# All pairs of heads in a written order on three engines; modulation sums kept out of the heads; the rotary swap on VectorE

## The chip, the cores and the metric

The kernel is one program on 1 core of one Trainium2 chip. The metric is the device time of one execution in microseconds (us); lower is better. Of the core's engines the text names TensorE (PE; its weight loads have a row of their own, PEld), VectorE (DVE), ScalarE (ACT), GpSimd (POOL) and SyncE (SP), which issues nearly all the loads. Before the change three runs took 1917.03 to 1919.51 us, with a median of 1918.83 us.

## The reference

The reference is a decoder trunk of two layers on one sequence of 256 tokens with 2048 features. Each layer has a mixer and a SwiGLU feed-forward network (FFN) with 5632 inner features. Shift, scale and gate of every sub-layer come from one conditioning vector c. Layer 0 mixes by pooling. After it, one set of keys and values is computed from a compressed latent of 512 features, and layer 1 attends to it with 16 heads of 128 + 64 features:

```python
for i in range(DEPTH):
    shift_m, scale_m, gate_m, shift_f, scale_f, gate_f = jnp.split(sc @ mod_w[i] + mod_b[i], N_MOD, axis=-1)
    if i == N_A:
        kv_shift, kv_scale = jnp.split(sc @ kv_mod_w + kv_mod_b, 2, axis=-1)
        h_kv = modulate(rmsnorm(x, kv_in_norm), kv_shift, kv_scale)
        kv = shared_kv(h_kv, w_dkv, kv_norm, w_uk, w_uv, w_kr, cos, sin)
    h = modulate(rmsnorm(x, norm_mix[i]), shift_m, scale_m)
    y = pool_mixer(...) if i < N_A else mla_mixer(h, kv, w_dq[j], q_norm[j], w_uq[j], w_o[j], cos, sin)
    x = x + gate_m[:, None, :] * y
    h = modulate(rmsnorm(x, norm_ffn[i]), shift_f, scale_f)
    x = x + gate_f[:, None, :] * swiglu(h, ffn_gate[i], ffn_up[i], ffn_down[i])
return rmsnorm(x, final_norm)
```

The rotary part of queries and of the shared key turns pairs of features: with t1 and t2 the halves of the 64, the result is (t1 cos - t2 sin, t2 cos + t1 sin).

## The kernel before

**Tiles and products.** A weight comes in units of 1 MB (a raw tile 128x2048). Each is split into an upper part, a rounded copy made by ACT (L374; L517 and L1362 are the same operation elsewhere), and a lower part, the rest, made by DVE (L376, L520, L1363). Activations are split in the same way, and a product is three products: upper by upper, upper by lower, lower by upper. One unit gives 24 matmuls of 128x512 on PE (L398).

**Stages.** The stages by time in the span are: pooling mixer and start of the modulation (0 to about 200 us), FFN of layer 0 (to about 890), a handover (to 938), then `keys_values(0..2)` with the first `hidden_q` (four pieces of the modulated hidden state, L540 and L558 to L560) and `w_dq` (to 998), `keys_values(3)` with the query latent (to 1010), the heads in 8 pairs (to 1098), the output projection `w_o` (to 1163), a second handover and the FFN of layer 1 (to the end).

**What sets the order.** Most of the program is ordered by a list scheduler from the written program, tile pools and priorities. Stretches inside `tc.manual_schedule(engines=ordered)` are kept as written on PE, ACT and DVE; in the kernel before, `then_attention` and the second handover are such stretches, and the heads aren't. Each engine runs its list in order: an instruction that waits holds all behind it. SP has such a list of loads too, and a load waits until the raw tile it fills has been used up.

**Modulation sums.** All but the first of the modulation matrices are reduced on DVE: a `Part` loads 1 MB and multiplies and sums it in one instruction (L211), 168 of them. They are a background list: `tick`, called once per weight unit, issues some of it at a rate that `plan(left, units)` or `release` sets, so that `left` remain after `units` ticks; `hold` stops it. When the last unit of a gate is in, the column is finished (L300), turned by PE (L292), copied by ACT (L294) and spread by DMA. `pending` holds work that `flush` issues at a later weight split.

**Handover.** Class `Handover` (L449 on) ends the FFN: the last down projection's products (L407), the last piece of the residual (L611, L612), the norm of that token half (ACT L427, DVE L470, POOL L472), scaling (L476; piece 0 on DVE, piece 1 on POOL), PE transposes (L482), modulated upper and whole parts (L490, L497, L499) and lower part (L503). `then_attention` continues with pieces 2 and 3 (L1183 to L1197), the key's rotary product (L1208, `key_part`) and the key latent (L1238 to L1253).

**Heads.** `project_heads(g)` loads and splits the query weights of two heads, makes the rotary product (12 matmuls, L1368 to L1370), copies it and its swapped halves by ACT (L843, four times L845), and the head products (L1288). `probabilities` is the softmax on ACT and DVE, `turned` transposes it (L1407), `output` multiplies it with the values. DVE finishes the rotation (L849, L850, L852).

## Time and profile before

| what | value |
|---|---|
| median of three runs | 1918.83 us (1917.03 to 1919.51) |
| profiled execution | 1918.19 us, of which the span is 1916.4 us |
| PE busy | 1862.8 us, 97% of the span |
| DVE busy | 1402.7 us, 73% |
| ACT busy | 850.2 us, 44% |
| DMA | 574.98 MB, mean 300 GB/s |

How to read it: the span is the time from the first to the last instruction, and the 1.8 us between span and execution time lie around it. Busy shares are means over stages with different limits, so a stage is read in a table of windows, and a wait is read in the timeline of one engine. There the columns are start, duration, engine, line, operation, output and inputs by the program's names, shapes and count. Where an engine stood idle first, square brackets give for how long and what ended it. Rows that follow on each other overlap a little, so a step is best read from one start to the next.

### The profile page before, as it was taken

How to read it: one execution, taken by the hardware profiler on the slowest of the kernel's cores; microseconds unless marked ns; L12 is line 12 of the kernel's file. 1: busy time of each engine (PE TensorE's matmuls, PEld its weight loads, DVE VectorE, ACT ScalarE, POOL GpSimd, SP SyncE). 2: the span in 40 equal slices, each digit the busy share in tenths (PEclk: the TensorE clock that was granted, in tenths of full speed). 3: DMA queues.
4: the chain of work that ended last, by engine and by line, in shares of the span. 5: the costliest groups of instructions: out<-in, count | busy, mean ns of one | idle time of the engine just before them, and what ended most of it. 6: DMA issues, size and time to landing. Idle time of an engine off the chain costs nothing.

```text
span 1916.4 us, 21930 instructions
## 1 busy us (share of the span) xinstructions
PE 1862.8 (97%) x8813; PEld 1507.8 (79%) x8813; DVE 1402.7 (73%) x1391; ACT 850.2 (44%) x958; POOL 26.9 (1%) x32
## 2 busy tenths in 40 slices
...
GB/s 399 398 418 417 368 364 333 319 299 361 357 344 332 327 330 326 332 373 274 212 371 291 293 278 194 397 318 335 260 284 240 241 240 239 249 222 205 220 198 44
DMA packets 86647, 574.98 MB, mean 300 GB/s; under 512 B 10977, under 2 KB 15505, under 8 KB 18321
## 3 DMA queue, kind: packets, MB, share of 16 engines
...
q14 instruction: 32, 0.26, 0.0%
q10 hardware_dynamic: 96, 0.02, 0.0%
...
## 4 chain that ended last, share of the span: by engine, by line
PE 69%; issue 22%; DMA 3%; DVE 3%; ACT 1%; SPq 0%; POOL 0%; POOLq 0%; DVEq 0%; ACTq 0%
PE ps L398 58%; DMA raw<-in_mod_w_dram 3%; PE ps L256 2%; PE ps L973 2%; PE ps L407 2%; PE ps L1288 2%; DVE raw L211 1%; PE ps L729 1%; PE ps L1197 1%; PE ps L540 0%; DMA raw<-in_mod_block_dram 0%; PE ps L196 0%; PE ps L948 0%; PE ps L770 0%; DVE hl L376 0%
## 5 line engine op out<-in xcount | busy, mean ns | idle before, releaser
L398 PE MATMUL ps<-hl,act 128*128 128x512 f32 x6744 | 1539.5, 390 | 1.9 <-DVE hl L376 1.0
L398 PEld LDWEIGHTS ps<-hl,act 128*128 128x128 f32 x6744 | 1263.0, 188 | 264.7 <-DVE hl L376 1.8
L376 DVE TENSOR_TENSOR hl<-raw,hl 128x2048 fp32r<-128x2048 f32 x289 | 661.1, 2289 | 253.2 <-ACT hl L374 252.5
L374 ACT ACTIVATE hl<-raw 128x2048 fp32r<-128x2048 f32 x289 | 553.1, 1918 | 647.8 <-PE ps L398 572.1
L211 DVE SCALAR_TENSOR_TENSOR raw<-raw,s_row 128x2048 f32<-128x2048 f32 x168 | 383.2, 2284 | 3.6 <-DMA raw<-in_mod_wt_dram 3.6
L256 PE MATMUL ps<-raw,s_strip 128*32 128x512 f32 x392 | 65.2, 760 | 34.6 <-DMA raw<-in_mod_w_dram 33.5
L698 DVE TENSOR_TENSOR act<-ps,act 128x512 f32<-128x512 f32 x96 | 64.5, 685 | 17.5 <-PE ps L398 17.5
L256 PEld LDWEIGHTS ps<-raw,s_strip 128*32 128x32 f32 x392 | 9.5, 121 | 70.0 <-DMA raw<-in_mod_w_dram 46.3
L784 DVE TENSOR_TENSOR x<-ps,x 128x512 f32<-128x512 f32 x32 | 22.1, 690 | 38.8 <-PE ps L398 38.8
L1288 PE MATMUL ps<-act,hl 128*128 128x256 f32 x384 | 49.6, 287 | 0.0
L1288 PEld LDWEIGHTS ps<-act,hl 128*128 128x128 f32 x384 | 48.3, 195 | 0.7 <-DVE act L1253 0.2
L407 PE MATMUL ps<-hl,act 128*128 128x512 f32 x192 | 47.0, 400 | 1.2 <-DVE act L503 1.2
L732 ACT ACTIVATE act<-ps 128x512 fp32r<-128x512 f32 x44 | 23.6, 594 | 50.0 <-PE ps L729 37.6
L407 PEld LDWEIGHTS ps<-hl,act 128*128 128x128 f32 x192 | 35.2, 188 | 10.7 <-ACT act L490 2.3
L263 DVE COPY t2k<-ps 128x256 f32<-128x256 f32 x4 | 1.7, 425 | 52.9 <-ACT t2k L262 52.9
L427 ACT ACTIVATE junk<-x 128x512 bf16<-128x512 f32 x23 | 14.5, 629 | 53.2 <-DVE x L612 37.6
L802 DVE TENSOR_TENSOR t2k<-ps,t2k 128x512 f32<-128x512 f32 x24 | 16.5, 689 | 28.5 <-PE ps L398 28.5
L798 ACT ACTIVATE t2k<-ps 128x512 f32<-128x512 f32 x24 | 14.2, 590 | 47.9 <-PE ps L398 47.9
L973 PEld LDWEIGHTS ps<-act,act 128*128 128x128 f32 x128 | 24.7, 200 | 11.6 <-issue 8.4
L696 ACT ACTIVATE act<-ps 128x512 f32<-128x512 f32 x32 | 19.1, 597 | 29.0 <-PE ps L398 28.8
L973 PE MATMUL ps<-act,act 128*128 128x256 f32 x128 | 31.9, 402 | 0.0
L733 DVE TENSOR_TENSOR act<-ps,act 128x512 fp32r<-128x512 f32 x44 | 28.1, 683 | 0.9 <-ACT act L732 0.9
...
## 6 DMA issues: line engine op xcount, KB each, us to landing
...
```

Of the source, the lines that this page charges most:

```text
L211: dve.scalar_tensor_tensor(out=r, in0=r, scalar=1.0, in1=s_row, op0=ALU.mult, op1=ALU.mult, accum_out=self.sums[:, self.n:self.n + 1])
L256: pe.matmul(self.bank[m * STRIP:(m + 1) * STRIP, :], lhsT=weights(k), rhs=r[:, k, i, :], start=first, stop=last)
L374: hi_ins = act.activation(hi, r, AF.Copy)
L376: lo_ins = dve.tensor_tensor(out=lo, in0=r, in1=hi.bitcast(F32), op=ALU.subtract)
L398: pe.matmul(banks[tok], lhsT=t_[:, i, k, tok * P:(tok + 1) * P], rhs=w[:, k, :], start=first and n < len(part), stop=last and n >= len(ord ...
L407: pe.matmul(bank, lhsT=t_[:, i, k, tok * P:(tok + 1) * P], rhs=w[:, k, :], start=first and n == 0, stop=last and n == len(order) - 1)
L698: dve.tensor_tensor(out=part, in0=banks[tok], in1=part, op=ALU.add)
L732: act.activation(m[:, 0, :, ts_], v, AF.Copy)
L733: dve.tensor_tensor(out=m[:, 1, :, ts_], in0=v, in1=m[:, 0, :, ts_].bitcast(F32), op=ALU.subtract)
L784: dve.tensor_tensor(out=x[:, tok, js], in0=banks[tok], in1=x[:, tok, js], op=ALU.add)
L973: pe.matmul(mixed[g][:, n % 2, :], lhsT=wp[g][:, k, ns], rhs=pool_all[g // 2][:, g % 2, k, :], start=k == 0, stop=k == KL - 1)
L1288: pe.matmul(pt[:, h, :], lhsT=w(h0 + h, k), rhs=t_[:, i, k, :], start=n == 0, stop=n == 3 * KL - 1)
```

## The change

1. The heads run in a written order: `heads_in_order` lays out scores, softmax in pieces (class `Softmax`), transposes, projection of pair g + 2, and `weighted` for pair g - 1, inside `manual_schedule`. The first units of the output projection run in halves of 12 matmuls around `weighted`. The query weights come as one contiguous tile per pair, rearranged on the host, with the rotary halves of the two heads in front.
2. The 16 units of the "mla" gate come ahead of the heads, and the heads have no ticks for modulation sums. Seven more units than before go into FFN 0, two more between the handover and the first rotary product; eight instead of five go into `w_o`.
3. The rotary swap goes by blocks of 64 rows and is made by DVE out of PSUM together with the sine product (two 64-row instructions and one cosine product); ACT's five copies are gone. `w_kr` comes as one contiguous 1 MB tile with the doubled columns in it.
4. ACT keeps plain copies of the transposed pieces 2 and 3 in the handover (`kept`, four copies of 128x512); `hidden_q` uses them, so 16 transposes are gone.
5. In the handover all scaling is on DVE, the first lower split is ahead of the first piece, and a step of the product order is exchanged. `hold` is one column earlier at the end of the FFN.
6. In the FFN the evacuation of a down product is put into `pending`, so it comes after the next split.

```diff
-FFN0_UNITS, MLA_UNITS, HEAD_UNITS, WO_UNITS, FFN1_UNITS = 95, 4, 16, 8, 60
+FFN0_UNITS, MLA_UNITS, DQ_UNITS, WO_UNITS, FFN1_UNITS = 93, 4, 5, 8, 60
-LATE, MLA_LATE, WO_LATE = 3, 5, 3
+LATE, MIX_LATE, MIX_DQ = 3, 14, 6
...
-            pending.append((0, spread))
+            pending.append((1, spread))
...
-            (dve if j == 0 else pool).tensor_scalar(out=self.turned[tok, j][0], in0=x[:, tok, j * CH:(j + 1) * CH],
-                                                    scalar1=self.rstd[:, tok:tok + 1], scalar2=None, op0=ALU.mult)
+            dve.tensor_scalar(out=self.turned[tok, j][0], in0=x[:, tok, j * CH:(j + 1) * CH],
+                              scalar1=self.rstd[:, tok:tok + 1], scalar2=None, op0=ALU.mult)
...
-                if last and j == ND - 1:
+                if last and j == ND - 2:
                     hold()
...
-                    elif i == 0:
-                        act.activation(x[:, tok, js], banks[tok], AF.Copy)
                     else:
-                        dve.tensor_tensor(out=x[:, tok, js], in0=banks[tok], in1=x[:, tok, js], op=ALU.add)
+                        pending.append((0, lambda bank=banks[tok], sums=x[:, tok, js]: gather(bank, sums, i == 0)))
...
-        act.activation(t_[:, 0, :], bank, AF.Copy)
-        for r in range(0, P, HALF):
-            act.activation(t_[r:r + HALF, 1, :], bank[r ^ HALF:(r ^ HALF) + HALF], AF.Copy)
+        for r in range(0, P, ROPE):
+            other = slice(r ^ ROPE, (r ^ ROPE) + ROPE)
+            dve.tensor_tensor(out=t_[r:r + ROPE, 1, :], in0=bank[other], in1=sin_t[other], op=ALU.mult)
+        dve.tensor_tensor(out=t_[:, 0, :], in0=bank, in1=cos_t, op=ALU.mult)
         return t_
     def rope_end(t_, dsts):
-        dve.tensor_tensor(out=t_[:, 1, :], in0=t_[:, 1, :], in1=sin_t, op=ALU.mult)
-        dve.tensor_tensor(out=t_[:, 0, :], in0=t_[:, 0, :], in1=cos_t, op=ALU.mult)
...
-    plan(n_all + MLA_LATE, FFN0_UNITS)
+    n_all -= n_mix
+    plan(n_all + MIX_LATE, FFN0_UNITS)
...
         split_upper(w[0])
+        split_lower(w[0])
         run(h.old(0))
...
-        run(b0[2], a1[2], b1[0], b1[1])
+        run(a1[2], b0[2], b1[0], b1[1])
...
+            for pt, dst in zip(pts, kept[-1]):
+                act.activation(dst, pt, AF.Copy)
...
-    release(n_all, MLA_UNITS)
+    release(n_all + MIX_DQ, MLA_UNITS)
...
-        pts = turned_pieces(pieces)
-        if len(hmx) < ND - 1:
+        pts = turned_pieces(pieces) if len(hmx) < 2 else kept[len(hmx) - 2]
+        if len(hmx) < 1:
             pieces = scaled(rstd, len(hmx) + 1)
...
-    plan(n_all - n_mix - WO_LATE, HEAD_UNITS)
+    plan(n_all, DQ_UNITS)
...
+        for g in range(pairs + 1):
+            if g < pairs:
+                sps = [scores(heads[g], h) for h in range(HG)]
+            if g >= 2:
+                behind[:] = [output(g - 2, banks.pop(g - 2)).ins]
+            if g < pairs:
+                soft[g] = [Softmax(sp) for sp in sps]
+                soft[g][0].masked()
...
+            if w:
+                split_upper(w)
+            if g < pairs:
+                soft[g][1].masked()
+            if g >= 1:
+                for s_ in soft[g - 1]:
+                    s_.turned()
+            if w:
+                split_lower(w)
+            if g + 2 < pairs:
+                heads.append(new_heads(g + 2))
+                t_ = rope_start(rope_products(*uq[g + 2]))
+            if g < pairs:
+                for s_ in soft[g]:
+                    s_.exponentials()
+            if g + 2 < pairs:
+                head_products(heads[g + 2], *uq[g + 2])
+            if g < pairs:
+                for s_ in soft[g]:
+                    s_.normed()
+            if g + 2 < pairs:
+                rope_end(t_, [(all_rows, heads[g + 2].qrT)])
+            run(fill[:half])
+            if g >= 1:
+                banks[g - 1] = weighted(heads[g - 1], soft.pop(g - 1))
+            run(fill[half:])
```

How the instructions move is shown at three places. The first is ACT around the transposes of `hidden_q(0)`, between the products of `w_uk` and `w_uv` of the third group of keys and values. The eight rows L558 and L559 make that piece's modulated whole and upper parts. Before, hl_6487 is the upper split of that group's `w_uv` and hl_6592 that of the first `w_dq`:

```order
L374 ACTIVATE hl_6487<-raw_6485 128x2048
L1280 ACTIVATE act_6283<-ps_6349 128x512
L374 ACTIVATE hl_6592<-raw_6586 128x2048
L1289 ACTIVATE act_6385<-ps_6400 128x512
L1289 ACTIVATE act_6385<-ps_6426 128x512
L558 ACTIVATE t2k_6467<-ps_6452,cols 128x256
L558 ACTIVATE t2k_6471<-ps_6452,cols 128x256
L559 ACTIVATE act_6466<-t2k_6467 128x256
L559 ACTIVATE act_6466<-t2k_6471 128x256
L558 ACTIVATE t2k_6475<-ps_6457,cols 128x256
L558 ACTIVATE t2k_6479<-ps_6457,cols 128x256
```

Now hl_6518 is the split of the same `w_uv`, and hl_6604 that of `w_dq`:

```order
L1297 ACTIVATE act_6415<-ps_6431 128x512
L1297 ACTIVATE act_6415<-ps_6457 128x512
L558 ACTIVATE t2k_6498<-ps_6483,cols 128x256
L558 ACTIVATE t2k_6502<-ps_6483,cols 128x256
L559 ACTIVATE act_6497<-t2k_6498 128x256
L559 ACTIVATE act_6497<-t2k_6502 128x256
L558 ACTIVATE t2k_6506<-ps_6488,cols 128x256
L558 ACTIVATE t2k_6510<-ps_6488,cols 128x256
L559 ACTIVATE act_6497<-t2k_6506 128x256
L559 ACTIVATE act_6497<-t2k_6510 128x256
L374 ACTIVATE hl_6518<-raw_6516 128x2048
L374 ACTIVATE hl_6604<-raw_6599 128x2048
```

On PE the first product with hl_6518 is still the next instruction after the eight transposes of `hidden_q(0)`; the two splits have gone from ahead of the eight ACT instructions to behind them.

The second place is where PE goes from the last group's `w_uv` (L398) to the first rotary product of the queries, on PE and on DVE. Before, PE:

```order
L398 MATMUL ps_6846<-hl_6855,act_6173 128x512 x8
L398 MATMUL ps_6846<-hl_6856,act_6173 128x512 x4
L1368 MATMUL ps_6896<-act_6836,hl_6891 128x256
L1369 MATMUL ps_6896<-act_6836,hl_6890 128x256
L1370 MATMUL ps_6896<-act_6836,hl_6890 128x256
```

and DVE ahead of that pair's rotation, where L1363 are lower splits of query weights and L1253 is the query latent's lower part:

```order
L211 SCALAR_TENSOR_TENSOR raw_6852,sums_6588<-raw_6852,s_row 128x2048
L1363 TENSOR_TENSOR hl_6891<-raw_6888,hl_6890 128x512
L1363 TENSOR_TENSOR hl_6891<-raw_6888,hl_6890 128x1024
L1253 SCALAR_TENSOR_TENSOR act_6836<-ps_6826,vcol,act_6836 128x256
L1363 TENSOR_TENSOR hl_6944<-raw_6941,hl_6943 128x512
L1253 SCALAR_TENSOR_TENSOR act_6836<-ps_6826,vcol,act_6836 128x256
L1363 TENSOR_TENSOR hl_6944<-raw_6941,hl_6943 128x1024
L1253 SCALAR_TENSOR_TENSOR act_6836<-ps_6831,vcol,act_6836 128x256 x2
L1363 TENSOR_TENSOR hl_7045<-raw_7039,hl_7044 128x512
L1363 TENSOR_TENSOR hl_7045<-raw_7039,hl_7044 128x1024
L850 TENSOR_TENSOR t2k_6909<-t2k_6909,cos_t 128x256
```

Now, PE, where L292 turns the column of the "mla" gate:

```order
L398 MATMUL ps_6848<-hl_6855,act_6199 128x512 x8
L398 MATMUL ps_6848<-hl_6856,act_6199 128x512 x4
L292 MATMUL ps_6893<-con,cols 16x128
L1370 MATMUL ps_6901<-act_6838,hl_6890 128x256
L1371 MATMUL ps_6901<-act_6838,hl_6889 128x256
L1372 MATMUL ps_6901<-act_6838,hl_6889 128x256
```

and DVE, where L300 finishes that column and L1459 are the lower splits of the first three pairs' query weights:

```order
L211 SCALAR_TENSOR_TENSOR raw_6851,sums_5661<-raw_6851,s_row 128x2048
L1261 SCALAR_TENSOR_TENSOR act_6838<-ps_6828,vcol,act_6838 128x256 x2
L1459 TENSOR_TENSOR hl_6890<-raw_6887,hl_6889 128x1536
L1261 SCALAR_TENSOR_TENSOR act_6838<-ps_6833,vcol,act_6838 128x256 x2
L1459 TENSOR_TENSOR hl_6948<-raw_6945,hl_6947 128x1536
L300 TENSOR_TENSOR cols<-sums_5661,vcol 128x16
L1459 TENSOR_TENSOR hl_6998<-raw_6995,hl_6997 128x1536
L850 TENSOR_TENSOR t2k_6914<-ps_6901,sin_t 64x256 x2
L851 TENSOR_TENSOR t2k_6914<-ps_6901,cos_t 128x256
```

The turn of the gate's column, which stood inside the heads, now stands right ahead of the first rotary product, and its column comes on DVE behind the second pair's lower split.

The third place is ACT at the end of the first pair's softmax, ahead of its transposes. Before, L1400 is the division for the second head, L1388 the scores of the next pair, L1409 the copies of turned probabilities:

```order
L1388 ACTIVATE t2k_7103<-ps_7098 128x128
L1362 ACTIVATE hl_7274<-raw_7269 128x1024
L1388 ACTIVATE t2k_7122<-ps_7117 128x128
L1409 ACTIVATE t2k_7140<-ps_7136 128x384
L1362 ACTIVATE hl_7393<-raw_7385 128x512
L1400 ACTIVATE t2k_7024<-t2k_7024,sm_7034 128x128
L1362 ACTIVATE hl_7393<-raw_7385 128x1024
L1409 ACTIVATE t2k_7146<-ps_7142 128x384
```

Now L1411 is the division for both heads, L1396 the next pair's scores, L1419 the copies:

```order
L1405 ACTIVATE t2k_7017,soft_7019<-t2k_7017,soft_7018 128x128
L1405 ACTIVATE t2k_7017,soft_7019<-t2k_7017,soft_7018 128x256
L1297 ACTIVATE act_7037<-ps_7059 128x512
L1411 ACTIVATE t2k_7013<-t2k_7013,soft_7016 128x128
L1411 ACTIVATE t2k_7017<-t2k_7017,soft_7020 128x128
L1396 ACTIVATE t2k_7102<-ps_7092 128x128
L517 ACTIVATE hl_7117<-raw_7115 128x1536
L1396 ACTIVATE t2k_7106<-ps_7097 128x128
L1419 ACTIVATE t2k_7129<-ps_7125 128x384
L1419 ACTIVATE t2k_7135<-ps_7131 128x384
```

The divisions of the first pair have gone ahead of the next pair's scores and weight split.

## The prediction

> **What bounds the kernel now.** I read the page first, then a table of windows by stage, then the timelines of PE, ACT, DVE and POOL where a window showed PE idle. The page's row of PE:

> ```profile
> PE 1862.8 (97%) x8813; PEld 1507.8 (79%) x8813; DVE 1402.7 (73%) x1391; ACT 850.2 (44%) x958; POOL 26.9 (1%) x32
> ```

> The windows (length, busy time of each engine with its instructions, granted clock, DMA share, GB/s):

> ```profile
> core 0: us, PE busy (x) PEld busy (x) DVE busy (x) ACT busy (x) POOL busy (x), PEclk, DMA share, GB/s
> 200.00:890.00 690.00, 689.85 (x3089) 571.99 (x3088) 577.14 (x479) 285.87 (x227) 0.70 (x1) 1.00 0.88 339
> 890.00:938.20 48.20, 44.37 (x231) 35.63 (x230) 35.70 (x51) 33.00 (x60) 16.39 (x10) 1.00 0.44 147
> 938.20:998.10 59.90, 59.86 (x346) 52.20 (x345) 57.04 (x62) 44.59 (x69) 0.55 (x1) 1.00 0.97 377
> 998.10:1010.30 12.20, 12.20 (x83) 11.14 (x82) 11.77 (x14) 9.11 (x17) 2.46 (x1) 1.00 0.87 303
> 1028.80:1098.00 69.20, 66.79 (x437) 61.08 (x437) 66.55 (x142) 57.25 (x150) 0.61 (x1) 0.98 0.73 268
> 1098.00:1163.00 65.00, 65.00 (x288) 53.79 (x288) 42.85 (x35) 27.40 (x25) 0.00 (x0) 1.00 0.72 270
> ```

> PE has work in nearly every microsecond from 200 on. Where the change acts, it can win only 48.20 - 44.37 = 3.8 us in the handover, 69.20 - 66.79 = 2.4 us in the heads, a stretch of lower clock there (0.98), and the time of products that are taken out. Between 938 and 1010 it can only lose by waits: PE is full, and DVE has 59.90 - 57.04 + 12.20 - 11.77 = 3.3 us to spare.

> **The handover: -2.5 us.** PE's three large waits there (idle time and what ended it in brackets):

> ```profile
> 900.41 0.66 PE L482 MATMUL ps<-con,t2k 128*128 128x128 f32 x4 [1.41 <-DVE t2k L476]
> 903.97 0.66 PE L482 MATMUL ps<-con,t2k 128*128 128x128 f32 x4 [0.80 <-POOL t2k L476]
> 912.88 1.88 PE L407 MATMUL ps<-hl,act 128*128 128x512 f32 x7 [1.18 <-DVE act L503]
> ```

> What lies ahead of the first two, on POOL and DVE:

> ```profile
> 899.93 3.98 POOL L476 TENSOR_SCALAR t2k<-x,rstd 128x512 f32<-128x512 f32 x1
> ...
> 894.28 2.29 DVE L211 SCALAR_TENSOR_TENSOR raw<-raw,s_row 128x2048 f32<-128x2048 f32 x1
> ...
> 899.87 0.49 DVE L476 TENSOR_SCALAR t2k<-x,rstd 128x512 f32<-128x512 f32 x1 [0.69 <-POOL rstd L472]
> ```

> The modulation sum at 894.28 stands ahead of L611, with which the chain to the first scaling begins. `hold` one column earlier takes it away: 2.3 us for a wait of 1.41, so all of that goes. POOL's 3.98 us become one more 0.49 on DVE: the 0.80 goes. The third wait hangs on the lower part (DVE L503), behind ACT's whole part and DVE's own; DVE now has the scalings too, so I give it 0.3 of 1.18. That is 1.41 + 0.80 + 0.3 = 2.5. Bounds: 0.8 (only the POOL part) and 3.4 (all three).

> **The kept copies: +0.8 us.** ACT makes two copies of 128x512 from PSUM more for each of two pieces. The nearest row is an evacuation of that shape; the others are ACT's rows around the second piece, and the upper parts of the key latent, which the products of the keys wait for:

> ```profile
> 1008.81 0.61 ACT L1280 ACTIVATE act<-ps 128x512 f32<-128x512 f32 x1
> ...
> 925.09 1.93 ACT L1183 ACTIVATE act<-ps,cols 128x256 fp32r<-128x256 f32 x4 [2.25 <-PE ps L540]
> ...
> 930.58 0.60 ACT L1238 ACTIVATE junk<-ps 128x512 bf16<-128x512 f32 x1 [0.76 <-PE ps L1197]
> ...
> 935.76 1.57 ACT L1251 ACTIVATE act<-ps,vcol 128x256 fp32r<-128x256 f32 x4
> ```

> The first piece's 1.2 us fall into the 2.25 in which ACT waits. Of the second piece's 1.2 the wait of 0.76 takes its part; 0.44 are left, and they reach the four latent rows at 935.76. The order also puts the split of the first `w_uv` among these four, so three of them come a split later, while PE has other products for most of it; for that I take another 0.4. In all 0.8. Bounds: 0 and 2.4 (4 x 0.61).

> **Transposes: -1.65 us.** Sixteen of the 128x128 transposes are gone. Eight run from one start to the next group's in 967.61 - 966.82 = 0.79 us, 0.10 each:

> ```profile
> 966.82 1.03 PE L540 MATMUL ps<-con,t2k 128*128 128x128 f32 x8
> 967.61 5.74 PE L398 MATMUL ps<-hl,act 128*128 128x512 f32 x24
> ```

> **The third group's keys and values: +5.95 us, and 1.5 for the clock.** The order puts the upper split of `w_uv` behind the eight ACT instructions of `hidden_q(0)`; PE needs it right behind the transposes. Before:

> ```profile
> 963.44 1.92 ACT L374 ACTIVATE hl<-raw 128x2048 fp32r<-128x2048 f32 x1
> ...
> 967.51 1.02 ACT L558 ACTIVATE t2k<-ps,cols 128x256 f32<-128x256 f32 x2
> ...
> 970.54 1.93 ACT L374 ACTIVATE hl<-raw 128x2048 fp32r<-128x2048 f32 x1
> ```

> The eight take 970.54 - 967.51 = 3.03 us, and start when the first four transposes are done, 0.4 before the last; then comes the split, 1.92, and about 0.2 to reach PE: 3.03 + 1.92 + 0.2 - 0.4 = 4.75 us in which PE has nothing else in its list. The lower split follows on DVE. For DVE and for PE ahead of this:

> ```profile
> 944.93 2.28 DVE L211 SCALAR_TENSOR_TENSOR raw<-raw,s_row 128x2048 f32<-128x2048 f32 x1
> ...
> 963.45 2.28 DVE L376 TENSOR_TENSOR hl<-raw,hl 128x2048 fp32r<-128x2048 f32 x1
> ...
> 961.06 5.92 PE L1288 MATMUL ps<-act,hl 128*128 128x256 f32 x48
> ```

> The lower split takes 2.28, while PE has 8 matmuls of 5.74 / 24 = 0.24, 1.9 us: 0.3 more, signals included. Nine sums instead of six now stand on DVE between the first group and this split, five of them ahead of the lower split of the third `w_uk`. From 944.93: the key's rotation 1.2, five sums and two splits 7 x 2.21, about 1 of waiting for ACT: 962.6. PE is at its first lower product at 961.06 + 8 x 0.12 = 962.0: with the signal 0.9 late, as all of these move with PE. In all 0.9 + 4.75 + 0.3 = 5.95. Bounds: 4.5 (the ACT chain without signals) and 8 (each of the sums' delays in full). What is late next is what stands behind, the four `w_dq` units; they find their splits ready, because in the wait DVE and ACT catch up.

> A halved clock follows such a wait once in this trace, the wait of 1.97 us in the heads (PE rows, and the window after it):

> ```profile
> 1030.81 0.55 PE L1407 MATMUL ps<-con,t2k 128*128 128x128 f32 x3 [1.97 <-ACT t2k L1400]
> ...
> 1032.69 0.41 PE L1368 MATMUL ps<-act,hl 128*128 128x256 f32 x1
> 1032.90 0.41 PE L1369 MATMUL ps<-act,hl 128*128 128x256 f32 x1
> ...
> 1031.70:1035.00 3.30, 3.30 (x18) 3.30 (x17) 3.30 (x9) 2.63 (x10) 0.00 (x0) 0.50 0.79 315
> ```

> For some 3.4 us these matmuls start every 0.21 us instead of 0.12: 3.4 x (1 - 0.12 / 0.21) = 1.5 us are lost. The waits of 1.41 and 1.18 had no such stretch (clock 1.00 in their window). A wait of 4.75 is over twice as long as the one that did it, so I add 1.5 once. [...]

> **The gate's column ahead of the first rotary product: +2.2 us.** L292 waits for L300 on DVE, behind the second lower split L1459, which waits for the second upper split on ACT, behind an evacuation that waits for the first half of `w_uv`. PE has the other half to do, 12 x 0.24 = 2.9 us. Against it stand the evacuation of 0.61, a split of 1536 columns on ACT and one on DVE, which before are done in two pieces each:

> ```profile
> 1009.45 1.58 ACT L1362 ACTIVATE hl<-raw 128x512 fp32r<-128x512 f32 x2
> ...
> 1008.05 0.68 DVE L1363 TENSOR_TENSOR hl<-raw,hl 128x512 fp32r<-128x512 f32 x1
> ...
> 1009.04 1.22 DVE L1363 TENSOR_TENSOR hl<-raw,hl 128x1024 fp32r<-128x1024 f32 x1
> ```

> 0.61 + 1.58 + 0.68 + 1.22 and 0.4 for L300 and signals (an estimate) are 4.5: PE waits 1.6. If DVE still carries one of the two sums that it has more by here, some 1.2 of its 2.28 are added, 2.8. I take the middle, 2.2, and no half clock; bounds 1.6 and 4.5 (with one).

> **Heads: -3.5 and -0.8 us.** Ahead of the wait of 1.97 ACT has a split in front of the division:

> ```profile
> 1029.83 0.64 ACT L1362 ACTIVATE hl<-raw 128x512 fp32r<-128x512 f32 x1
> 1030.35 0.41 ACT L1400 ACTIVATE t2k<-t2k,sm 128x128 f32<-128x128 f32 x1
> ...
> L845 ACT ACTIVATE t2k<-ps 32x256 f32<-32x256 f32 x20 | 7.5, 375 | 0.3
> L211 DVE SCALAR_TENSOR_TENSOR raw<-raw,s_row 128x2048 f32<-128x2048 f32 x11 | 25.1, 2283 | 0.0
> ```

> Now the division is ahead of it, DVE has no sums in between (25.1 us less), and ACT loses its swaps. So this wait goes, with its half clock: 1.97 + 1.5 = 3.5. The later waits are small:

> ```profile
> 1068.34 0.33 PE L1407 MATMUL ps<-con,t2k 128*128 128x128 f32 x1 [0.26 <-ACT t2k L1400]
> 1078.06 0.70 PE L1414 MATMUL ps<-t2k,act 128*128 128x256 f32 x2 [0.17 <-ACT t2k L1409]
> ```

> They go too, 0.43, and about as much again in starts that come late without an idle row (an estimate): 0.8. Bounds for the heads together: 2.5 and 5.

> **Costed at nothing.** Seven more sums in FFN 0 are 7 x 2.28 = 16 us of DVE in a stage where it has 690 - 577 = 113 us free, and 7 MB on some 234 (339 GB/s x 690 us). Evacuations that come behind the next split hold their banks for 2.3 us longer; PE's 689.85 of 690 leave nothing to win and, if a bank were missing at each down product, 10 us and more to lose. Three more sums in `w_o` find 65 - 42.85 = 22 us of DVE. The swap on DVE adds 0.42 us a pair (two 64-row instructions and a cosine for a sine and a cosine), against 3 us a pair from the sums. The larger `w_kr` adds half a MB in a window with a DMA share of 0.44.

> **The sum.** -2.5 + 0.8 - 1.65 + 5.95 + 1.5 + 2.2 - 3.5 - 0.8 = +2.0. From the profiled execution, 1918.19 us (the span of 1916.4 and 1.8 around it, which stay), that gives 1920.2 us. The profiled execution stands 0.6 below the median shown, 1918.83. A measurement tells about 0.2% (3.8 us) from no change, so this is no change.

> **Rivals.**
> - *Faster.* The waits cost only themselves. The handover gives 3.4 instead of 2.5, the copies hide (-0.8), the third `w_uk` isn't late and the lower split comes in time (-1.2), the clock holds (-1.5), the gate's column costs 1.6 (-0.6), the heads give 0.7 more: 5.7 less, 1914.5. For it: DVE is less loaded in the heads and before; against it: the window 938 to 998 has no slack that would hide three of these.
> - *Slower.* DVE and the queue behind it decide from 945 on. It has 3.3 us to spare up to 1010 and gets two more sums, 4.4 us, and three more than now ahead of the first `hidden_q`; loads wait for the raw tiles these free, with DMA at 0.97. If DVE stays behind through `w_dq`, its lower splits come 1 us late three times, the wait at L292 is 3 and its clock is halved too: 3 x 1 + 0.8 + 1.5 = 5.3 more, 1925.5. It decides once DVE's backlog at the first `w_dq` unit is over 1.8 us, the 8 matmuls that PE can do without the lower split.
> - *It doesn't do what it says.* The scheduler's order keeps the waits in the heads, as ACT's scores of the next pair still depend on PE; then the heads' 4.3 are not won: 1924.5 with the two new waits, some 1917 if the scheduler's times were as wrong for those.

> **How the numbers follow.** The forecast has 0.45: 0.35 of it within 0.2%, 0.08 slower, 0.02 faster; its own range is 1916 to 1925. The faster rival has 0.27, the slower 0.20, the last 0.08 (half within, half slower). Faster 0.29, same 0.39, slower 0.32. The range reaches from beyond the faster rival's value, 1911.5, to beyond the slower one's, 1927.

> **What would show it.** In the changed profile, right: no bracket at L482 over 0.3 us; an idle of 4 to 5 us on PE ahead of the third `w_uv` (L398), released by ACT L374; a PE idle of 1.5 to 3 at L292; a half-clock stretch near 975 and none near 1030; DVE near full from 945 to 1010. Wrong: PE idle by less than 2 us at that `w_uv`, new idle time in FFN 0, or brackets above 0.5 us inside the heads.

## The result, and the profile after

The changed kernel takes 1927.97 us (median of five runs, 1927.82 to 1928.14). The kernel before, run beside it, takes 1918.76 us (five runs, 1914.87 to 1919.51). The ratio is 1.0052, with a 95% interval from 1.0041 to 1.0063: slower by 0.5%, 1 us beyond the upper end of the predicted range. The profiled execution takes 1927.86 us, 9.67 more than the one of before.

The page's row of busy times, after:

```profile
PE 1863.2 (97%) x8797; PEld 1508.1 (78%) x8797; DVE 1412.7 (73%) x1394; ACT 830.0 (43%) x904; POOL 20.9 (1%) x30
```

PE is busy for as long as before (1862.8 us); the span has grown from 1916.4 to 1926.1 us. So the time is idle time of PE. (Stretches in which its clock is halved count as busy: the 4.00 us at a mean clock of 0.57 further down are all busy.) The windows of the stages, after (the first is FFN 0, then the handover, the stretch to `w_dq`'s end, the query latent, the heads):

```profile
core 0: us, PE busy (x) PEld busy (x) DVE busy (x) ACT busy (x) POOL busy (x), PEclk, DMA share, GB/s
200.00:895.00 695.00, 692.06 (x3089) 571.19 (x3088) 593.10 (x494) 286.23 (x226) 0.70 (x1) 1.00 0.89 349
895.00:943.70 48.70, 45.38 (x235) 36.37 (x234) 35.73 (x52) 32.98 (x62) 10.35 (x8) 1.00 0.39 138
943.70:1010.50 66.80, 61.08 (x343) 53.43 (x344) 63.72 (x67) 41.12 (x64) 2.06 (x1) 0.97 0.96 371
1010.50:1022.50 12.00, 10.22 (x65) 8.89 (x63) 10.84 (x14) 9.95 (x14) 0.95 (x2) 1.00 0.80 273
1041.00:1107.00 66.00, 65.54 (x443) 60.50 (x442) 53.22 (x123) 47.62 (x123) 0.00 (x0) 1.00 0.36 133
```

PE now idles 2.9 us in FFN 0, where it idled 0.15; 3.3 in the handover, where it was 3.8; and 5.7 and 1.8 in two stretches that had none. The heads' idle time is down from 2.4 us to 0.46, and DVE has 53.22 of 66 us there where it had 66.55 of 69.

Every wait of PE of 0.4 us or more between 600 and 1125 us of the timeline, after (three dots stand for two rows that are like the first):

```profile
634.99 5.78 PE L398 MATMUL ps<-hl,act 128*128 128x512 f32 x24 [0.45 <-ACT hl L374]
...
835.90 22.10 PE L398 MATMUL ps<-hl,act 128*128 128x512 f32 x96 [0.45 <-ACT hl L374]
875.12 15.52 PE L398 MATMUL ps<-hl,act 128*128 128x512 f32 x66 [0.56 <-DVE hl L376]
891.22 3.48 PE L398 MATMUL ps<-hl,act 128*128 128x512 f32 x14 [0.58 <-DVE hl L376]
906.42 0.66 PE L482 MATMUL ps<-con,t2k 128*128 128x128 f32 x4 [1.74 <-DVE t2k L476]
914.92 2.56 PE L407 MATMUL ps<-hl,act 128*128 128x512 f32 x10 [0.88 <-DVE hl L520]
968.00 5.06 PE L1296 MATMUL ps<-act,hl 128*128 128x256 f32 x40 [1.07 <-DVE hl L376]
978.59 7.36 PE L398 MATMUL ps<-hl,act 128*128 128x512 f32 x24 [4.65 <-ACT hl L374]
1022.69 0.28 PE L292 MATMUL ps<-con,cols 128*16 128x128 f32 x1 [1.97 <-DVE cols L300]
1105.21 0.88 PE L1417 MATMUL ps<-con,t2k 128*128 128x128 f32 x6 [0.46 <-ACT t2k L1411]
```

The first stands four times (the two rows left out are at 680 and 725). It has an idle row of 0.45, but from PE's last start before it 0.73 us more than usual pass; for 875 and 891 that is 0.83 and 0.85.

To see where the time goes, take one PE instruction at the border of each stage and compare its start in the two timelines:

| from … to | before, us | after, us | difference | forecast |
|---|---|---|---|---|
| start … first unit of FFN 0 | 169.39 | 169.97 | +0.58 | 0 |
| … first product of the handover (L407) | 719.39 | 724.57 | +5.18 | 0 |
| … first product of the keys | 49.17 | 48.47 | -0.69 | -1.7 |
| … first rotary product | 72.21 | 79.71 | +7.50 | +8.0 |
| … first scores | 8.63 | 10.20 | +1.57 | 0 |
| … second pair's softmax transposes | 22.12 | 18.46 | -3.67 | -3.5 |
| … second handover | 122.01 | 121.22 | -0.78 | -0.8 |
| … end | 745.15 | 745.15 | 0.00 | 0 |

The first row isn't the change's: up to there the mean DMA share is 1.00 in both profiles (407 and 405 GB/s) and PE is busy for 131.47 of 169.39 us before and 129.81 of 169.97 after, and in the runs below it is -1.5 to +1.2 us without an edit in it. Three rows are off: FFN 0 by much, the 1.57 us behind the first rotary product, and the handover by 1.0. The 1.57 us are a second stretch of half clock. The windows behind the waits of 4.65 and 1.97 us, after:

```profile
978.00:983.00 5.00, 4.41 (x12) 3.53 (x13) 4.80 (x7) 2.34 (x2) 0.00 (x0) 0.66 1.01 421
1023.00:1027.00 4.00, 4.00 (x23) 4.00 (x22) 3.08 (x5) 0.27 (x1) 0.00 (x0) 0.57 0.99 347
```

### The profile page after: what moved, and what is told of

Read it like the earlier page. It is cut to its first block, busy times and chain, and to the rows that moved or that the text cites. A ratio compares the mean times of both kernels' runs of the same rounds, so it can differ in the third digit from the quotient of the medians.

```text
span 1926.1 us, 21857 instructions
## 1 busy us (share of the span) xinstructions
PE 1863.2 (97%) x8797; PEld 1508.1 (78%) x8797; DVE 1412.7 (73%) x1394; ACT 830.0 (43%) x904; POOL 20.9 (1%) x30
## 3 DMA queue, kind: packets, MB, share of 16 engines
q8 instruction: 69, 1.13, 0.2%
## 4 chain that ended last, share of the span: by engine, by line
PE 90%; DMA 4%; DVE 3%; ACT 1%; issue 1%; SPq 0%; POOL 0%; POOLq 0%; DVEq 0%; ACTq 0%
PE ps L398 75%; DMA raw<-in_mod_w_dram 3%; PE ps L256 2%; PE ps L1296 2%; PE ps L977 2%; PE ps L407 2%; DVE hl L376 1%; PE ps L729 1%; DVE raw L211 1%; PE ps L1475 1%; ACT hl L374 1%; PE ps L1208 1%; DMA raw<-in_mod_block_dram 0%; DMA raw<-in_w_uk_dram 0%; PE ps L196 0%
## 5 line engine op out<-in xcount | busy, mean ns | idle before, releaser
L398 PE MATMUL ps<-hl,act 128*128 128x512 f32 x6672 | 1526.9, 390 | 8.6 <-ACT hl L374 6.5
L398 PEld LDWEIGHTS ps<-hl,act 128*128 128x128 f32 x6672 | 1251.7, 188 | 272.1 <-ACT hl L374 8.4
L376 DVE TENSOR_TENSOR hl<-raw,hl 128x2048 fp32r<-128x2048 f32 x286 | 653.8, 2289 | 247.9 <-ACT hl L374 247.3
L374 ACT ACTIVATE hl<-raw 128x2048 fp32r<-128x2048 f32 x286 | 546.6, 1918 | 604.1 <-PE ps L398 433.8
L211 DVE SCALAR_TENSOR_TENSOR raw<-raw,s_row 128x2048 f32<-128x2048 f32 x168 | 383.0, 2285 | 2.0 <-DMA raw<-in_mod_wt_dram 2.0
L407 PE MATMUL ps<-hl,act 128*128 128x512 f32 x192 | 47.0, 398 | 1.1 <-DVE hl L520 0.9
L802 ACT ACTIVATE t2k<-ps 128x512 f32<-128x512 f32 x24 | 14.2, 590 | 71.7 <-PE ps L398 71.7
L407 PEld LDWEIGHTS ps<-hl,act 128*128 128x128 f32 x192 | 35.2, 188 | 10.6 <-ACT act L490 1.5
L520 DVE TENSOR_TENSOR hl<-raw,hl 128x2048 fp32r<-128x2048 f32 (+2 forms) x16 | 31.8, 1987 | 5.7 <-ACT hl L517 5.7
```

Source lines behind the costliest of these rows:

```text
L211: dve.scalar_tensor_tensor(out=r, in0=r, scalar=1.0, in1=s_row, op0=ALU.mult, op1=ALU.mult, accum_out=self.sums[:, self.n:self.n + 1])
L374: hi_ins = act.activation(hi, r, AF.Copy)
L376: lo_ins = dve.tensor_tensor(out=lo, in0=r, in1=hi.bitcast(F32), op=ALU.subtract)
L398: pe.matmul(banks[tok], lhsT=t_[:, i, k, tok * P:(tok + 1) * P], rhs=w[:, k, :], start=first and n < len(part), stop=last and n >= len(ord ...
L407: pe.matmul(bank, lhsT=t_[:, i, k, tok * P:(tok + 1) * P], rhs=w[:, k, :], start=first and n == 0, stop=last and n == len(order) - 1)
L520: dve.tensor_tensor(out=w[2][:, ks], in0=w[0][:, ks], in1=w[1][:, ks].bitcast(F32), op=ALU.subtract)
```

## The experiments

The times of each are set against the kernel before on the same chip; "FFN 0", "handover" and so on are the rows of the table above, worked out in the same way. Where no ratio is given, the kernel ran once, and its time has no interval.

**FFN 0: the sums alone, and the late evacuations alone.** The first experiment is the kernel before with seven more sums in FFN 0, the second the kernel before with the down products' evacuations put behind the next split, the third the changed kernel without that.

```diff
-LATE, MLA_LATE, WO_LATE = 3, 5, 3
+LATE, MLA_LATE, WO_LATE = 3, -2, 3
```

> The kernel before with one number changed: seven more modulation sums in FFN 0 (105 instead of 98, so fewer between the handover and the output projection). Theory A, the sums make FFN 0's waits: four waits of about 0.7 us at a split behind a Silu and two of about 0.85 at a DVE split, FFN 0 4 to 5 us longer than before, whole time about 1922. Theory B, the deferred evacuations make them: FFN 0 as long as before, whole time within 2 us of 1918.8.

```diff
-                    elif i == 0:
-                        act.activation(x[:, tok, js], banks[tok], AF.Copy)
                     else:
-                        dve.tensor_tensor(out=x[:, tok, js], in0=banks[tok], in1=x[:, tok, js], op=ALU.add)
+                        pending.append((0, lambda bank=banks[tok], sums=x[:, tok, js]: gather(bank, sums, i == 0)))
```

> The kernel before with one part of the change alone: the evacuations of FFN down products are deferred behind the next split. Theory A (the sums make FFN 0's waits): no waits in FFN 0, whole time within 2 us of 1918.8. Theory B (the deferral makes them): FFN 0 4 to 5 us longer, about 1923.5.

> The changed kernel without the deferral of the FFN down evacuations. The sums alone had cost FFN 0 2.95 us, all of the change 5.2. Theory A, the rest too is DVE's load near the end of FFN 0 (more sums per unit, since the stop comes a column earlier): FFN 0 stays at +5.2 within 0.5. Theory B, the deferral costs the rest once DVE is full: +3.

The sums alone: 1922.96 us, ratio 1.0023 (1.0013 to 1.0033). FFN 0 is +2.95, less than the 4 to 5 that theory A had: three of the four waits at a split on ACT are there (634.66, 679.84 and 725.02), the two on DVE at the end of the stage aren't. A new wait stands in the handover, where the last lower split comes late (PE's timeline with the sums alone):

```profile
896.78 8.46 PE L407 MATMUL ps<-hl,act 128*128 128x512 f32 x36 [2.75 <-DVE hl L376]
```

The evacuations alone: 1917.91 us, ratio 0.9992 (0.9983 to 1.0002), FFN 0 +0.01. The changed kernel without them: 1927.96 us, FFN 0 +5.16. So the evacuations cost nothing. It is the sums, and from 2.95 to 5.18 it is the sums together with the earlier `hold`, which leaves them one column less of the stage: that `hold` with 98 sums makes none of these six waits either (below).

**How seven sums cost FFN 0 5 us when DVE has 100 us free.** ACT's timeline around the wait at 634.99, after:

```profile
632.53 0.60 ACT L802 ACTIVATE t2k<-ps 128x512 f32<-128x512 f32 x1 [14.18 <-PE ps L398]
633.03 1.91 ACT L374 ACTIVATE hl<-raw 128x2048 fp32r<-128x2048 f32 x1
634.83 0.59 ACT L802 ACTIVATE t2k<-ps 128x512 f32<-128x512 f32 x1
```

The same place before:

```profile
621.21 1.92 ACT L374 ACTIVATE hl<-raw 128x2048 fp32r<-128x2048 f32 x1 [3.52 <-PE ps L398]
626.65 1.92 ACT L374 ACTIVATE hl<-raw 128x2048 fp32r<-128x2048 f32 x1 [3.52 <-PE ps L398]
631.18 0.60 ACT L798 ACTIVATE t2k<-ps 128x512 f32<-128x512 f32 x1 [2.62 <-PE ps L398]
633.90 0.60 ACT L798 ACTIVATE t2k<-ps 128x512 f32<-128x512 f32 x1 [2.12 <-PE ps L398]
```

L802 (L798 before) are the two Silus of a gate chunk, one for each token bank. After, ACT stands idle for 14.18 us until the first bank is finished, and the split that PE needs next stands behind the first Silu, although its weight, issued at 615.73, had landed 4.8 us later. It then starts 1.5 us before PE wants it and takes 1.91. Before, two splits have been done ahead of the Silus. The scheduler has changed the order because of the sums: no engine was short of time. ACT did not take the split ahead of the Silu that waited: 12.5 us pass from the landing of its weight (620.53) to its start (633.03), and ACT does nothing in them but that Silu.

The test writes the two Silus of the changed kernel in the other order, the bank that is finished last first:

```diff
-            nat[c] = []
-            for tok in range(NT):
-                sg = t2k([P, CH])
+            nat[c] = [t2k([P, CH]) for _ in range(NT)]
+            for tok in reversed(range(NT)):
+                sg = nat[c][tok]
                 act.activation(sg, gb[tok], AF.Silu)
-                nat[c].append(sg)
```

> The changed kernel, with the two Silus of a gate chunk written in the other order (the second token's bank, which is finished last, first), in both FFNs. In ScalarE's written order they then stand side by side again, with no split of a weight between them, although FFN 0 still holds 105 sums. Theory A (of FFN 0's +5.18 us, the four waits of 0.73 us over their usual length come from a split that stands between the two Silus and is kept by the second until TensorE's next bank is done; the two waits of 0.8 us at 875 and 891 us and what follows them come from VectorE's sums): the four waits are gone, FFN 0 costs +2.3 us (5.18 - 4 x 0.73), the time is 1925.0 us. Theory B (VectorE's load alone makes all six; a split that comes earlier on ScalarE is then late on VectorE): FFN 0 stays between +4.7 and +5.7 us, the time between 1927.4 and 1928.5 us. The bank that is read last is now read 0.6 us later, in FFN 1 as well, where 0 to 0.5 us is expected of that by both.

1924.68 us, ratio 1.0034 (1.0022 to 1.0046): 3.3 us less than the changed kernel. PE's timeline of it around 634, and the first wait that is left:

```profile
599.81 40.51 PE L398 MATMUL ps<-hl,act 128*128 128x512 f32 x178
...
873.24 15.53 PE L398 MATMUL ps<-hl,act 128*128 128x512 f32 x66 [0.56 <-DVE hl L376]
```

The four waits are gone, the two on DVE stay, and FFN 0 is +3.10, 2.1 less where 2.9 were expected. What is missing isn't in the waits. In this execution the clock was halved over the stage's first 6 us; in the changed kernel's profile it was so for half as long. The first 6 us of FFN 0 in the changed kernel, and in the one with the Silus turned (PE's clock is the number behind POOL's):

```profile
169.97:175.97 6.00, 6.00 (x20) 4.82 (x21) 5.86 (x12) 3.22 (x4) 0.00 (x0) 0.73 1.01 416
```

```profile
170.14:176.14 6.00, 6.00 (x14) 4.74 (x15) 5.86 (x12) 3.22 (x4) 0.00 (x0) 0.50 1.02 419
```

What goes with it is read at the start of the 97th product of the stage, set against the kernel before, whose clock was full there: +0.01 us in the changed kernel, +1.12 with the Silus turned. The 3.41 us of half clock in the changed kernel (0.50 from 169.75 to 173.16) cost no more by that product, as they take the place of two short waits for DVE's splits (0.38 and 0.58 us in the kernel before); the 6 us go with +1.12 here and with +1.13 in the run of the handover alone. That run has 98 sums and the Silus in the old order, this one 105 and the Silus turned, so it isn't these edits that choose. Behind that start FFN 0 is +1.98 instead of +5.17. So 3.2 us are ACT's order, four waits of 0.73 and a little more; 1.7 of the rest are the two waits on DVE (0.83 + 0.85) at the last splits. The run with the sums alone doesn't have these two, nor has the one with the earlier `hold` and 98 sums: it takes both.

Most of what remains of the 3.3 us in the whole time is the half clock at L292, which this profile doesn't have though its wait is 1.96 (clock 1.00 from 1021.2 to 1028; see the end).

**The handover alone.** The kernel before with the change's edits of the handover and `hold` one column earlier, without anything else:

```diff
-            (dve if j == 0 else pool).tensor_scalar(out=self.turned[tok, j][0], in0=x[:, tok, j * CH:(j + 1) * CH],
+            dve.tensor_scalar(out=self.turned[tok, j][0], in0=x[:, tok, j * CH:(j + 1) * CH],
...
-                if last and j == ND - 1:
+                if last and j == ND - 2:
                     hold()
...
+        split_lower(w[0])
         run(h.old(0))
...
-        split_lower(w[0])
         fs = h.old(1)
...
-        run(b0[2], a1[2], b1[0], b1[1])
+        run(a1[2], b0[2], b1[0], b1[1])
```

> The kernel before with the handover's edits alone (all scaling on DVE, first lower split ahead of the first piece, the exchanged step, the stop of the sums a column earlier). My prediction's term for it: handover 2.5 us shorter (2 to 3), whole 1917. Rival, DVE gets in each other's way there whatever the sums do: less than 1 us shorter, 1918.5 or more.

1918.79 us, ratio 1.0006 (0.9997 to 1.0015). The handover is -2.62, as forecast (-2.5). What it won went elsewhere: the sums that `hold` pushed on cost +2.10 ahead of the first rotary product, and the later heads +1.75. FFN 0 is +1.16, but +1.13 of it is the half clock over the stage's first 6 us in this execution, so the earlier `hold` alone costs nothing there. (The second pair comes 2.03 earlier, with a wait of 1.42 where it was 1.97 and no half clock behind it: 1.00 from 1031.5 to 1039.) In the changed kernel the handover is only -0.69, because DVE comes into it late: the last sums of FFN 0 push its splits and residual adds back, and the wait at L482 is 1.74, where it is 0.49 with 98 sums and the rest of the change, and gone with the handover's edits alone.

**The third group's keys and values.** First the changed kernel with the hidden state's transposes ahead of the third `w_uk`, so that the split of `w_uv` gets its time on ACT:

```diff
-        head_T(kT, KG, lambda h, k: hi[:, k, h * P:(h + 1) * P], lambda h, k: lo[:, k, h * P:(h + 1) * P], ckvT)
         if between:
             between()
+        head_T(kT, KG, lambda h, k: hi[:, k, h * P:(h + 1) * P], lambda h, k: lo[:, k, h * P:(h + 1) * P], ckvT)
```

> The changed kernel, with the transposes of hidden_q(0) ahead of the third group's w_uk products instead of between these and w_uv. Theory A, the split's place behind ACT's eight instructions makes the wait of 4.65 us: these now run under PE's products, and only an evacuation (0.6) and the split (1.9) with signals are left, a wait of 2.7; 1926, or 1924.5 if the clock stays up. Theory B, the late load or DVE's sums make it: the wait stays between 4 and 5, 1928.

1929.43 us, ratio 1.0050 (1.0035 to 1.0064): no gain; the stretch to the first rotary product is +11.78 instead of +7.50, and the 1.57 behind it are gone. PE's waits in it from 930 us on:

```profile
974.94 2.11 PE L398 MATMUL ps<-hl,act 128*128 128x512 f32 x8 [2.48 <-ACT hl L374]
979.64 5.53 PE L398 MATMUL ps<-hl,act 128*128 128x512 f32 x16 [2.58 <-DVE hl L376]
1011.04 0.66 PE L540 MATMUL ps<-con,t2k 128*128 128x128 f32 x2 [3.23 <-DVE sm L1247]
```

One wait on ACT became a smaller one, as theory A had it (2.7), and two on DVE. So DVE is late there as well. The 2.48 that stay on ACT come from the load of `w_uv`: it was issued at 964.05 and took 8.8 us to land, and the split starts 0.1 us after that, at 972.99. In the changed kernel the same load came as late. Its issue, its time from issue to landing, and ACT's splits of `w_uv` and `w_dq`:

```profile
965.06 0.33 SPq L387 DMA_DIRECT2D raw<-in_w_uv_dram  x1
...
raw<-in_w_uv_dram SPq DMA_DIRECT2D x1, 1024.0 KB, 8.5
...
976.62 3.72 ACT L374 ACTIVATE hl<-raw 128x2048 fp32r<-128x2048 f32 x2
```

So it landed at 973.57, 0.4 us before PE was through with its transposes (972.91 + 1.03). Of the 4.65 us, 3.05 (973.57 to 976.62) are ACT's order; about 1.6 would have stayed with any order, as the split takes 1.92. In the kernel before, this load was issued at 952.50. Next, three sums fewer between the handover and the first hidden state (six instead of nine). The last three of the sixteen tiles of the layer 1 mixer's gate are left out of the computation for it.

> The changed kernel with three sums fewer between the handover and the first hidden_q (6 instead of 9); the last 3 of the 16 tiles of the mla gate are left out of the computation. Theory A, DVE's backlog of sums sets the wait at the third w_uv: the wait of 4.65 us falls under 1.5, the 1.07 at the third w_uk goes, the clock stays up. Theory B, the order on ACT alone sets it: the wait stays at 4 to 5.

Its single run took 1917.21 us, without a wait of PE at that `w_uv`. The stretch to the first rotary product is -2.47 instead of +7.50, and the 1.57 behind it are gone: three sums, 6.9 us of DVE, cost 11.5 us. But this took away three things: DVE's time, 3 MB of loads, and with them ACT's order, which the scheduler wrote anew (the split of `w_uv` ahead of the eight copies of the hidden state). Two runs take them apart in part. In one, three of the nine sums cover 64 of 2048 columns, the loads stay, and so does ACT's order; in the other, three sums work on the tile that the sum before has used, so three loads go and DVE's time stays. The gate's values are then others.

```diff
+            js = slice(0, 64 if self.n in self.special else D)
-            dve.scalar_tensor_tensor(out=r, in0=r, scalar=1.0, in1=s_row, op0=ALU.mult, op1=ALU.mult,
+            dve.scalar_tensor_tensor(out=r[:, js], in0=r[:, js], scalar=1.0, in1=s_row[:, js], op0=ALU.mult, op1=ALU.mult,
```

> The changed kernel, with three of the nine sums between the handover and the first hidden state for the queries (tiles 3, 5 and 7 of the gate of layer 1's mixer) multiplied over 64 of their 2048 columns only: the 1 MB loads stay, some 6.6 us of VectorE go (3 x (2.29 - 0.08)). The order of ScalarE is the changed kernel's there: the upper split of the third w_uv stands behind the eight copies of the hidden state. The output of these tiles' gate leaves the other columns out. Theory A (the written order of ScalarE makes the wait at the third w_uv, VectorE's sums make the others): the 4.65 us there stay (4 to 5), the 1.07 ahead of it and the 1.97 at the gate's column are gone or under 0.6, no half clock behind the latter, and from the handover to the first rotary product it is +4 to +5.5 us instead of +7.50. Theory B (VectorE's backlog makes all three): the wait at the third w_uv is under 2 us as well, and the stretch at +1 us or less. Theory C (the loads, which move at some 420 GB/s there, make them): the three waits stay within 0.5 us, and the stretch at +6.5 to +8 us.

```diff
-            r = raw_t([P, D])
-            sync.dma_start(r, self.w[self.tiles[self.n] * P:(self.tiles[self.n] + 1) * P, :])
+            if self.n not in self.special:
+                self.r = raw_t([P, D])
+                sync.dma_start(self.r, self.w[self.tiles[self.n] * P:(self.tiles[self.n] + 1) * P, :])
+            r = self.r
```

> The changed kernel, with the same three sums made over a tile that the sum before has just used, so that VectorE has all nine sums and three loads of 1 MB are left out (the gate of layer 1's mixer is computed from other tiles there). ScalarE's order changes with it: the upper split of the third w_uv now stands ahead of the copies of the hidden state. Theory A (ScalarE's order, VectorE's sums): no wait of over 1.5 us on ScalarE at the third w_uv, but waits on VectorE of 2 to 4 us in all by the first rotary product, the wait at the gate's column (1.97 us, within 0.7) among them; from the handover to the first rotary product +1 to +4 us. Theory B (VectorE's backlog makes all): waits of 5 us and more in all, +5.5 us or more. Theory C (the loads): no waits, -2 us or less, as with three sums fewer altogether.

The two ran once each, 1925.37 us with the short sums and 1922.36 with the loads left out; the kernel before took 1915.51 beside them. PE's waits from 930 us on with the short sums:

```profile
975.38 8.11 PE L400 MATMUL ps<-hl,act 128*128 128x512 f32 x24 [4.65 <-ACT hl L376]
1020.22 0.28 PE L294 MATMUL ps<-con,cols 128*16 128x128 f32 x1 [1.96 <-DVE cols L302]
```

And with the loads left out:

```profile
1002.20 5.06 PE L1300 MATMUL ps<-act,hl 128*128 128x256 f32 x40 [1.09 <-DVE hl L379]
1010.07 0.44 PE L543 MATMUL ps<-con,t2k 128*128 128x128 f32 x2 [2.81 <-DVE sm L1251]
1018.61 0.27 PE L295 MATMUL ps<-con,cols 128*16 128x128 f32 x1 [0.36 <-DVE cols L303]
```

With 6.2 us less on DVE (the three sums took 0.22 us each instead of 2.29) and ACT's order kept, the 4.65 us stay and so does the wait at the gate's column (1.96); only the 1.07 at the third `w_uk` is gone (stretch +7.06, more than theory A's +4 to +5.5, as the gate's wait stayed and the 24 products behind the 4.65, part of them at half clock, took 8.11 us here instead of 7.36). So the two large waits aren't the time of these three sums. In the other run ACT's order is another, DVE has all nine sums, and the third `w_uv` lands at 966.50: the 4.65 is gone, and DVE's waits come to 1.09 + 2.81 + 0.36 (stretch +4.00, the upper end of theory A). Both mechanisms of the forecast are real: an order that holds the split back, and a backlog of DVE that costs some 4 us as soon as the order lets it through. Nine sums bring both, six neither. What the three loads do alone isn't shown, as no run leaves them out with ACT's order kept.

The 1.07 at the third `w_uk` is not DVE's backlog alone. In the changed kernel's profile ACT waits there for the load of `w_uk`, and DVE for ACT's split:

```profile
963.70 1.92 ACT L374 ACTIVATE hl<-raw 128x2048 fp32r<-128x2048 f32 x1 [2.56 <-DMA raw<-in_w_uk_dram]
...
965.66 2.29 DVE L376 TENSOR_TENSOR hl<-raw,hl 128x2048 fp32r<-128x2048 f32 x1 [0.62 <-ACT hl L374]
```

That load took 7.8 us to land. In the next run, with all nine sums and the same order up to there, it took 5.2, ACT and DVE have no such wait, and PE has none at that `w_uk`.

**The gate's column and the half clock.** The changed kernel with L292 and its copy in the second pair of heads:

```diff
-            pending.append((1, spread))
+            pending.append((1 if name != "mla" else 9, spread))
...
+            if g == 1:
+                flush()
             run(fill[:half])
```

> The changed kernel, with the turn of the mla gate's column (L292) moved from ahead of the first rotary product to the second pair of heads. Theory A: the wait of 1.97 us there goes and with it the half-clock stretch that follows, 3.5 us less: 1924.5. Theory B, the first pair's splits are as late as the column: a wait of over 1 us stays at the first rotary product, and the time is less than 1.5 us lower.

1923.43 us, ratio 1.0025 (1.0015 to 1.0034), 4.5 us less than the changed kernel. The stretch to the first rotary product is +4.77 instead of +7.50, and the +1.57 behind it is 0. By these rows it is 4.3 us, and 1.97 + 1.57 = 3.5 are the column's, as theory A had it; the rest is the 1.07 at the third `w_uk`, which this execution doesn't have, less a half clock that lasts longer behind the wait at the third `w_uv` (4.66; its 24 products took 7.97 us here and 7.36 in the changed kernel).

**Where the sums can go.** The last six runs keep the change and spread the sums otherwise; two of them also turn the Silus. First: 98 in FFN 0 as before the change, seven in the pairs of heads, the gate's column in `w_o`.

```diff
-LATE, MIX_LATE, MIX_DQ = 3, 14, 6
+LATE, MIX_LATE, MIX_DQ = 3, 21, 13
...
-            pending.append((1, spread))
+            pending.append((1 if name != "mla" else 0, spread))
...
+            pump(1)
...
-    plan(n_all, DQ_UNITS)
+    plan(n_all + 7, DQ_UNITS)
...
+            pump((1, 3, 5, 6, 7, 8, 8).count(g))
```

> The changed kernel with its sums spread differently and nothing left out: 98 in FFN 0 as before the change, 2 in the handover behind the modulated pieces, 7 up to the first hidden_q, 6 up to the first rotary product, 7 inside the pairs of heads (pairs 1, 3, 5, 6, 7 and two in the last round), the column's turn in the output projection. Theory A, DVE's load of sums makes the waits in FFN 0, at the third w_uv and at the first rotary product: FFN 0 within 0.5 us of before, under 1 us of waits at the third w_uv, none at the first rotary product, and the whole 6 to 7 us below the kernel before: 1912 to 1914. Theory B, the other parts (deferral, copies, swap) make them: the waits stay, and the sums in the heads add theirs: 1925 or more.

1916.51 us, ratio 0.9993 (0.9985 to 1.0002). FFN 0 is +0.77, the handover -1.95, the stretch to the first rotary product -2.53 without a wait; all of that is given back at one place, behind the heads (+4.61): an idle row of 3.78 us, 3.94 by the starts, with half clock behind it (a mean of 0.55 from 1102.2 to 1105.6). PE's timeline there, and DVE's:

```profile
1102.16 0.28 PE L292 MATMUL ps<-con,cols 128*16 128x128 f32 x1 [3.78 <-DVE cols L300]
```

```profile
1095.31 2.28 DVE L211 SCALAR_TENSOR_TENSOR raw<-raw,s_row 128x2048 f32<-128x2048 f32 x1
...
1097.52 2.29 DVE L211 SCALAR_TENSOR_TENSOR raw<-raw,s_row 128x2048 f32<-128x2048 f32 x1
...
1101.93 0.17 DVE L300 TENSOR_TENSOR cols<-sums,vcol 128x16 f32<-128x16 f32 x1
```

Taking the two sums of pair 8 to the query's first projections instead (five in the heads, eight there), without and with the other order of the Silus:

```diff
-    plan(n_all + 7, DQ_UNITS)
+    plan(n_all + 5, DQ_UNITS)
...
-            pump((1, 3, 5, 6, 7, 8, 8).count(g))
+            pump((1, 3, 5, 6, 7).count(g))
```

> The kernel with the sums spread again (98 sums in FFN 0, 2 in the handover, 7 before the first hidden state for the queries), with five sums in the pairs of heads (pairs 1, 3, 5, 6, 7) instead of seven (1, 3, 5, 6, 7, 8, 8), and the two that this takes out put with the query's first projections, which then hold 8. The gate's column transpose stays in the output projection. Theory A (the 3.94 us wait at that transpose, and the half clock behind it, come from the last two sums standing on VectorE right ahead of the column): the wait is gone, the part from the first transpose of weights of the second pair to the second handover falls from +4.61 us to between 0 and +0.7, the time is 1912.2 us (1916.5 - 4.3), faster than both kernels. Theory B (VectorE is full there as elsewhere, so two sums that are taken out of the last pairs come back as waits before the first rotary product): from the handover to the first rotary product it is +1 to +3 us instead of -0.58, and the time 1914.5 to 1917 us.

> The kernel with five sums in the heads, and the two Silus of a gate chunk in the other order. With 98 sums in FFN 0, one of the four waits of 0.7 us is left by the written order (a split between two Silus in two of the chunks instead of the seven). Theory A (the split between the Silus is what costs): 0.5 to 0.8 us less than the kernel with five sums and the old order, 1911.6 us if that one has 1912.2. Theory B (it is VectorE's load): no difference to it, within 0.3 us.

1919.12 us, ratio 1.0007 (0.9998 to 1.0016), and 1918.96 us, 1.0008 (0.9999 to 1.0016). The wait at L292 is gone (behind the heads -0.65), as theory A had it, but the stretch to the first rotary product is +5.51 and +5.84, beyond what either theory had (with seven in the heads that row was -2.53, not -0.58). DVE's timeline with five in the heads, and the wait of PE:

```profile
992.60 2.28 DVE L211 SCALAR_TENSOR_TENSOR raw<-raw,s_row 128x2048 f32<-128x2048 f32 x1
...
994.88 2.28 DVE L211 SCALAR_TENSOR_TENSOR raw<-raw,s_row 128x2048 f32<-128x2048 f32 x1
...
997.59 0.75 DVE L1250 TENSOR_SCALAR t2k<-ps,sm 128x512 f32<-128x512 f32 x1 [0.43 <-POOL sm L1249]
```

```profile
1000.43 2.07 PE L1297 MATMUL ps<-act,hl 128*128 128x256 f32 x8 [4.46 <-ACT hl L374]
```

Two sums stand ahead of the query latent's norm, and the split that PE waits for stands on ACT behind the norm. The Silus' order changes nothing here, as FFN 0 with 98 sums has none of the four waits (+0.77 and +0.76). Last, one sum in each of pairs 1 to 7; then six in the heads with 99 in FFN 0; then that with the other order of the Silus:

```diff
-            pump((1, 3, 5, 6, 7, 8, 8).count(g))
+            pump((1, 2, 3, 4, 5, 6, 7).count(g))
```

```diff
-LATE, MIX_LATE, MIX_DQ = 3, 21, 13
+LATE, MIX_LATE, MIX_DQ = 3, 20, 12
...
-    plan(n_all + 7, DQ_UNITS)
+    plan(n_all + 6, DQ_UNITS)
...
-            pump((1, 3, 5, 6, 7, 8, 8).count(g))
+            pump((1, 2, 4, 5, 6, 7).count(g))
```

> The kernel with seven sums in the pairs of heads, one in each of pairs 1 to 7 instead of in 1, 3, 5, 6, 7, 8 and 8; nothing else is different. Theory A (it is the place: the two sums of pair 8 stand on VectorE right ahead of the gate's column, which TensorE waits for): the 3.94 us wait at the gate's column transpose is gone, the heads are -0.8 to 0 us instead of +4.61, and the time is 1912.2 us. Theory B (it is the number: VectorE has 6.9 us of work in a round of 8.5 us, and a sum in each makes 9.2 us, so that it falls 0.7 us further behind in each round): waits of 1 to 4 us come somewhere else in pairs 4 to 8, some with half clock behind them, and the time stays between 1914.5 and 1918 us.

> Six sums in the pairs of heads (1, 2, 4, 5, 6, 7), and one more in FFN 0 (99); six with the query's first projections as in the kernel with seven in the heads. Theory A (the place): -0.8 to 0 us in the heads, FFN 0 +0.3 to +1.5 instead of +0.77, no wait before the first rotary product, the time 1912.7 us. Theory B (the number): six rounds that fall 0.7 us behind with three between that catch up 1.6 us each fit, so the waits in the heads are under 1 us, and the time is 1913 to 1914 us. A and B differ with the kernel that has one in each of seven pairs: by B this one is at least 2 us faster than that.

> The kernel with six sums in the heads and 99 in FFN 0, and the two Silus of a gate chunk in the other order. The written order of the one without has a split between the two Silus in a chunk of FFN 0 that has none with 98 sums. By the theory of the Silus 0.5 to 0.8 us less than without; by the theory of VectorE's load no difference within 0.3 us.

| sums in the heads | us | ratio to before (95%) | FFN 0 | to first rotary product | behind second pair |
|---|---|---|---|---|---|
| 7, two in pair 8 | 1916.51 | 0.9993 (0.9985 to 1.0002) | +0.77 | -2.53 | +4.61 |
| 7, one each | 1911.78 | 0.9967 (0.9956 to 0.9978) | +0.78 | -2.52 | -0.25 |
| 6 | 1911.92 | 0.9970 (0.9959 to 0.9981) | +2.05 | -2.53 | -0.63 |
| 6, Silus turned | 1910.42 | 0.9962 (0.9949 to 0.9976) | +0.80 | -2.52 | -0.62 |

It is the place: seven in the heads cost no more than half a microsecond over six once none stands right ahead of the column, and six are no faster. The last has the lowest median, 0.4% under the kernel before and some 17 us under the change as it was made; the intervals of the last three overlap. The difference of 1.25 us in FFN 0 between the last two is mostly not the Silus': 0.97 of it is the half clock over the stage's first units (0.52 there in one profile, 1.00 in the other), which leaves 0.28 for them, where 0.5 to 0.8 were expected. The last one's page:

```profile
PE 1857.7 (97%) x8797; PEld 1505.0 (79%) x8797; DVE 1411.0 (74%) x1394; ACT 830.5 (44%) x904; POOL 20.9 (1%) x30
```

The engines do the same work as in the changed kernel (DVE 1412.7, ACT 830.0); only PE's busy time, which holds the stretches of half clock, is 5.5 us shorter.

## Why the prediction was wrong

It said 1920.2 us, no change, and the time is 1927.97. By its profiled execution the sum missed 7.7 us, and they lie in few steps.

- **"Costed at nothing": the step that failed.** "Seven more sums in FFN 0 are 7 x 2.28 = 16 us of DVE in a stage where it has 690 - 577 = 113 us free." The work has room, yet it costs 5.18 us (alone 2.95 there, and 2.75 as a wait just behind). A mean over 690 us says nothing about which instruction stands behind which: the new order put a split behind a Silu at four places (3.2 us, as the run with the Silus turned shows), and the sums made DVE late at the stage's end, once `hold` ended them a column earlier. The part of the same step on the evacuations was right; three more sums in `w_o` and the swap fit too, as the heads came out at -3.67 and -0.78 for -3.5 and -0.8.
- **The handover: -2.5 and +0.8.** Right for the edits alone (-2.62), and -1.95 with the kept copies and 98 sums in FFN 0, so the copies cost about what was said, together with two sums that this run puts there. In the changed kernel it is -0.69, as the sums of FFN 0 reach into it: the step took DVE's list at the stage's end from the trace of before.
- **The third group: +5.95.** Measured 1.07 for 0.9, 4.65 for 4.75; the 0.3 at the lower split doesn't show. The 4.65 ended where the forecast said, at the split behind the eight on ACT, and stayed with short sums; but the load of `w_uv`, which the step left out, would have kept some 1.6 of it. The 0.2 for reaching PE was the author's estimate; here PE starts 0.05 us after the split's end (978.54 to 978.59). The 1.07 is partly luck: it hangs on a load that took 7.8 us in this execution. The sum had "about 1 of waiting for ACT" on DVE, and DVE did wait 0.38 + 0.62, but for splits that waited for loads.
- **The clock, +1.5 once.** It was halved twice behind waits. The one at the third `w_uv` was counted (24 products took 7.36 us there instead of 5.74, so 1.6); the one behind the gate's column, +1.57, was left out ("and no half clock") although the trace of before showed such a stretch behind 1.97 us, and the forecast wait was 2.2.
- **The gate's column: +2.2.** 1.97, near the value that was taken, and 3.5 with its half clock.
- **Transposes and heads: -1.65, -3.5, -0.8.** The heads measured -3.67 and -0.78. Some 1.5 to 2 of the -3.67 hang on the profiled execution of the kernel before, whose clock was halved there: in the three runs that have the old heads, without that half clock, the same row is -1.47, -2.04 and -2.03. The stretch that holds the transposes measured +7.50 for +8.0, and 1.07 + 4.65 + 1.6 + 1.97 less 1.65 for them is 7.6.

Of the rivals, the slower one had DVE's backlog decide from 945 on, with three late splits in `w_dq`. PE has no wait in `w_dq`; from that rival only the half clock at the gate's column came true. Its time, 1925.5, is nearer than the forecast's, but for another reason: none of the cases had FFN 0.

Of what was to show the steps right, the profile has the idle time of 4 to 5 us at the third `w_uv`, that of 1.5 to 3 at L292, the half clock near 975 and none near 1030, and DVE near full from 943.70 to 1010.50 (63.72 of 66.80); it doesn't have quiet waits at L482 (1.74). Of what was to show the sum wrong, it has new idle time in FFN 0, and no wait above 0.5 inside the heads (0.46).

Open stay why the clock is halved for 3.41 us at the start of FFN 0 in some executions, for some 6 in others and not at all in the rest, and what of the waits at the third group goes back to the loads alone.
